# A two-FFN decoder layer with seven-product matrix steps: more of them per chunk, and their closing sums ranked later

## The chip, the cores and the metric

The kernel runs on one core of a Trainium2 chip. The metric is the device time of one execution, in microseconds (us).

## The reference, cut to what matters

One decoder layer over 256 tokens of width 2048, in float32. The two FFNs hold most of the work:

```python
def swiglu(h, w_in, w_out):
    gu = h @ w_in
    gate, up = gu[..., :D_FF], gu[..., D_FF:]
    return (jax.nn.silu(gate) * up) @ w_out

h = h + 0.5 * swiglu(rmsnorm(h, ffn1_norm), ffn1_w_in, ffn1_w_out)
...   # pooling mixer and gated linear attention, h = h + concat(...) @ w_out_mix
h = h + 0.5 * swiglu(rmsnorm(h, ffn2_norm), ffn2_w_in, ffn2_w_out)
return rmsnorm(h, final_norm)
```

D_FF is 5632, so `w_in` is 2048 x 11264 and `w_out` 5632 x 2048.

## The kernel before, in words

**Three matmuls per product.** Every float32 operand is split into a high part (rounded to the matmul's type) and a low part (what is left). A product of two blocks is three matmuls: high x high, low x high and high x low (`three`, line 191, all 128 x 128 by 128 x 512 in the FFNs).

**Steps.** The weights come in loads of 1 MB, each with four blocks of 128 x 512: two blocks of rows by a gate and an up column block (or two column blocks of `w_out`). One load is one step. An ordinary step (S) multiplies the four blocks with the activations of both token halves: eight products, 24 matmuls. A seven-product step (W) is the Winograd form of the same 2 x 2 block product: seven products, 21 matmuls. It pays in vector work. An S step's four blocks go through ScalarE (copy to the high part, line 155) and VectorE (subtract to the low part, line 156). A W step needs seven split blocks (B11, B22, B21 and T1 to T4), and VectorE first forms the T blocks by three subtractions in place (line 179). The sums of activations that a W step multiplies with (`s_f`, `s_z`) are made once per FFN for six of the eight steps.

**Chunks.** `w_in` is worked in 11 chunks of 512 gate and 512 up columns (`first_product`), eight steps each. `KINDS` gives the kinds of the steps by chunk: FFN 1 is named "f", FFN 2 "z". The rows of `CHUNKS` hold for chunks 3 to 10. Between chunks stands a stretch of the second product with `w_out` (`second_product`), as a rule two earlier chunks: four S steps. `GROUPS` sets that alternation.

**PSUM.** A chunk's own sums are two tiles (`ps_fi`, `ps_zi`, one for each token half, in the notation below ps_zi4_0 and ps_zi4_1 for chunk 4). W steps add two more tiles, which collect the products that several outputs share: p16 and p75 in the code, pw_zi4_0 and pw_zi4_1 in names. With them a chunk holds all of PSUM. The second product that follows (`ps_fo`, `ps_zo`) takes the two shared tiles, the first one as its first tile.

**The closing sums.** After the last W step of a chunk `combine` reads the shared tiles: one ScalarE copy (line 297) and four VectorE additions (lines 298 to 301, 128 x 512 each) make `add_fi` or `add_zi`. The copy and the addition of line 298 free the first shared tile. Line 483 then adds the result to the chunk's own sums, lines 490 and 492 gate, line 499 transposes on TensorE, and lines 504 and 505 split the hidden values.

**What sets the order.** The program is written in one stream. A scheduler ranks each instruction by a priority that grows as the code is written, and lays out each engine's order from the ranks and from when it reckons inputs to be ready. At run time each engine takes its instructions in that order; semaphores hold one until its inputs are there. The split blocks lie in rings (22 blocks in all during an FFN), the raw loads in four 1 MB buffers, so ScalarE, VectorE and the loads can run ahead of TensorE only so far.

Of the kernel before, what the change touches and what calls it, by code (L numbers as in the profile page):

```python
# [57 lines left out]


W_PAIRS = (1, 3, 4, 6, 2, 5)  # L60
CHUNKS = ("WWSWWWSS", "WWWWWWSS") * 3 + ("WWSWWWSS",) * 2
KINDS = {
    "f": ("SSSSSSSS", "SSSSSSSS", "WWSWWWSS") + CHUNKS,
    "z": ("SSSSSSSS", "SWSWWWSS", "WWSWWWSS") + CHUNKS,
}
# [10 lines left out]
WIDE = True  # L76
ROW_AT = 7
S_AT = 3
MIX_BLOCKS = 9


@with_exitstack
def layer(ctx: ExitStack, tc: tile.TileContext, io):
# [83 lines left out]
    def s_step(src, parts=1, runs=WIDE):  # L167

        w = load(src, parts=parts).rearrange("p (b c) -> p b c", c=CW)
        b = parts_of(w, SINGLES if parts == 4 else PAIRS if parts == 2 or not WIDE else ALL)  # L170
        return lambda k, n: b[n if k == 0 else 3 - n]

    def w_step(src):

        w = load(src).rearrange("p (b c) -> p b c", c=CW)
        f = dict(zip(("B11", "B22", "B21"), parts_of(w, (slice(0, 1), slice(2, 4)))))

        def less(out, x, y):
            nc.vector.tensor_tensor(out=out, in0=x, in1=y, op=ALU.subtract)  # L179


        less(w[:, 0:2, :], w[:, 1:2, :].broadcast_to([P, 2, CW]), w[:, 0:4:2, :])
        less(w[:, 2, :], w[:, 2, :], w[:, 0, :])
        less(w[:, 3, :], w[:, 3, :], w[:, 2, :])
        f.update(zip(("T1", "T3", "T2", "T4"), parts_of(w, PAIRS)))
        return f

    def three(ps, a, b, start, stop, **kw):

        for i, (x, y) in enumerate(((a[0], b[0]), (a[0], b[1]), (a[1], b[0]))):  # L190
            nc.tensor.matmul(ps, x, y, start=start and i == 0, stop=stop and i == 2, **kw)  # L191

    class Group:
# [66 lines left out]
        def w(self, a, s, b):  # L260

            if self.one is None:
                self.one = [
                    self.psum[self.tags[1]].tile(
                        [P, 2, CW], F32, tag=self.tags[1], name=f"pw_{self.name}_{i}"
                    )
                    for i in range(2)
                ]
                first = True
            else:  # L270
                first = False
            self.left_w -= 1
            last = self.left_w == 0
            p16, p75 = self.one
            for (t, n), x, y in (((0, 0), a(0, 1), b["B21"]), ((0, 1), s["S4"], b["B22"])):
                ps, start, stop = self.target(t, n)
                three(ps, x, y, start, stop)
            three(p16[:, 0, :], a(0, 0), b["B11"], first, last)
            three(p75[:, 1, :], s["S1"], b["T1"], first, last)
            three(p75[:, 0, :], s["S3"], b["T3"], first, last)  # L280
            three(p16[:, 1, :], s["S2"], b["T2"], first, last)
            ps, start, stop = self.target(1, 0)
            three(ps, a(1, 1), b["T4"], start, stop)
            self.n += 1
            if last:
                self.combine()

        def combine(self):

            p16, p75 = self.one  # L290
            self.add = [
                ftmp[0].tile([P, 2, CW], F32, tag=f"add{t}", name=f"add_{self.name}_{t}")
                for t in range(NT)
            ]
            c, d = self.add
            u2 = d[:, 1, :]
            nc.scalar.copy(out=c[:, 0, :], in_=p16[:, 0, :])
            nc.vector.tensor_tensor(out=u2, in0=p16[:, 1, :], in1=c[:, 0, :], op=ALU.add)
            nc.vector.tensor_tensor(out=c[:, 1, :], in0=p75[:, 1, :], in1=u2, op=ALU.add)
            nc.vector.tensor_tensor(out=d[:, 0, :], in0=p75[:, 0, :], in1=u2, op=ALU.add)  # L300
            nc.vector.tensor_tensor(out=d[:, 1, :], in0=p75[:, 1, :], in1=d[:, 0, :], op=ALU.add)
# [133 lines left out]
    def ffn(psum, spool, act, pair, w_in, w_out, row, name, finish, first=None, behind=None):  # L435
# [10 lines left out]
        def a_of(kp):  # L446
            def a(t, k):
                hi, lo = act(2 * kp + k)
                return hi[:, t * P : (t + 1) * P], lo[:, t * P : (t + 1) * P]
            return a  # L450
# [5 lines left out]
        def first_product(c):  # L456
# [4 lines left out]
            for i, kind in enumerate(kinds):  # L461
# [4 lines left out]
                else:  # L466
# [6 lines left out]
                    grp.s(a_of(kp), b)  # L473
                if c == 0 and i >= S_AT:
                    for k in W_PAIRS:
# [207 lines left out]
    mixc = mix_sb.enter_context(tc.tile_pool(name="mixc", bufs=1, reuse_waits="tile"))  # L683
    blk = mix_sb.enter_context(tc.tile_pool(name="blk", bufs=MIX_BLOCKS, reuse_waits="tile"))

# [446 lines left out]
```

## Time and profile before

| | |
|---|---|
| median of 3 runs | 1710.91 us (1709.63 to 1710.96) |
| the profiled execution | 1711.71 us |
| its span, first to last instruction | 1709.9 us |
| TensorE (PE) busy | 1697.0 us, 7732 records |
| weight loads (PEld) busy | 1410.6 us |
| VectorE (DVE) busy | 1375.2 us |
| ScalarE (ACT) busy | 979.7 us |
| GpSimd (POOL) busy | 68.5 us |
| DMA | 365.22 MB, mean 214 GB/s |

Times within the trace count from the start of the span. FFN 1 lies from 0 to about 700 us, the mixer to about 1000 us, FFN 2 from there to the end. [...] In a timeline row stand the start, the duration, the engine, the line, the operation, out<-in, and in brackets the engine's idle time before it with what ended it.

### The profile page before, as it was taken

To read this page: it belongs to the slowest core of one execution; us is meant where nothing else is said; L and a number is where in the kernel's file an instruction comes from. 1 tells how busy PE (TensorE), PEld (TensorE's weight loads), DVE (VectorE), ACT (ScalarE), POOL (GpSimd) and SP (SyncE) were. 2 spreads that over 40 slices of the span, in tenths; PEclk is the share of its full clock that TensorE was granted. 3 is DMA by queue.
4 is the path that set the end of the run, shared out by engine and by line. 5 is a ranking of instruction groups with operands and counts; after the bars stand their busy time and mean duration, and the time that the engine had idled before them with its cause. 6 is when DMAs were issued, how large, how long until landed. Compare 5 with 4: busy or idle time off the path is not lost.

```text
span 1709.9 us, 20097 instructions
## 1 busy us (share of the span) xinstructions
PE 1697.0 (99%) x7732; PEld 1410.6 (82%) x7732; DVE 1375.2 (80%) x1483; ACT 979.7 (57%) x1220; POOL 68.5 (4%) x70
## 2 busy tenths in 40 slices
PE   9999999999999999999999999999999999999997
PEld 7888888888888888888988888888888888888886
DVE  8778899998899986644464677999998988998973
ACT  6655566565566564563454464656556556656542
POOL 0000000000000000000000000000000000000122
PEclk9999999999999999999999999999999999999999
DMA  9845756756756666454564664566667566567671
GB/s 354 335 123 222 265 153 246 271 150 238 252 172 228 239 224 231 171 182 142 191 216 170 213 235 145 190 253 208 210 222 243 176 225 243 182 236 249 200 289 49
DMA packets 60017, 365.22 MB, mean 214 GB/s; under 512 B 6785, under 2 KB 9985, under 8 KB 21266
## 3 DMA queue, kind: packets, MB, share of 16 engines
q1 hardware_dynamic: 51810, 335.61, 53.9%
q0 software_dynamic: 7392, 27.27, 7.5%
q8 instruction: 60, 0.98, 0.2%
q10 hardware_dynamic: 720, 1.07, 0.2%
q14 instruction: 35, 0.29, 0.0%
HBM read 338.75 MB, written 25.17 MB: 213 GB/s over the span
## 4 chain that ended last, share of the span: by engine, by line
PE 99%; issue 0%; ACT 0%; DMA 0%; POOL 0%; DVE 0%; POOLq 0%; ACTq 0%
PE ps_fi L191 19%; PE ps_zi L191 18%; PE ps_fo L191 14%; PE ps_zo L191 14%; PE pw_zi L191 8%; PE pw_fi L191 8%; PE ps_h L191 5%; PE ps_mp L191 3%; PE ps_mv L191 3%; PE ps_mg L191 2%; PE ps_mq L191 1%; PE ps_w_mk L191 1%; PE ps_w_mgr L191 1%; PE ftp L499 1%; PE ztp L499 1%; PE tp_h L428 0%
## 5 line engine op out<-in xcount | busy, mean ns | idle before, releaser
L156 DVE TENSOR_TENSOR ring_lo<-ring_raw,ring_hi 128x1024 fp32r<-128x1024 f32 (+5 forms) x426 | 550.2, 1304 | 213.2 <-ACT ring_hi L155 212.4
L155 ACT CAST ring_hi<-ring_raw 128x1024 fp32r<-128x1024 f32 (+3 forms) x511 | 480.9, 963 | 361.5 <-DMA ring_raw<-in_ffn_w_out 48.1
L179 DVE TENSOR_TENSOR ring_raw<-ring_raw 128x512 f32<-128x512 f32 (+1 forms) x213 | 182.2, 862 | 1.0
L191 PE MATMUL ps_zi<-ring_lo,h_hi 128*128 128x512 f32 x312 | 121.5, 389 | 0.0
L191 PE MATMUL ps_zi<-ring_hi,h_lo 128*128 128x512 f32 x312 | 121.1, 389 | 0.0
L191 PE MATMUL ps_zi<-ring_hi,h_hi 128*128 128x512 f32 x312 | 120.4, 389 | 0.0
L191 PE MATMUL ps_fi<-ring_lo,xT_hi 128*128 128x512 f32 x286 | 112.5, 393 | 0.0
L191 PE MATMUL ps_fi<-ring_hi,xT_lo 128*128 128x512 f32 x286 | 111.4, 392 | 0.0
L191 PE MATMUL ps_fi<-ring_hi,xT_hi 128*128 128x512 f32 x286 | 109.6, 393 | 1.9 <-ACT ring_hi L155 1.9
L191 PE MATMUL ps_fo<-ring_lo,fhi 128*128 128x512 f32 x278 | 109.2, 393 | 0.0
L191 PE MATMUL ps_fo<-ring_hi,flo 128*128 128x512 f32 x278 | 108.5, 392 | 0.0
L191 PE MATMUL ps_fo<-ring_hi,fhi 128*128 128x512 f32 x278 | 107.6, 391 | 0.0
L155 ACT CAST ring_hi<-fring_raw 128x1024 fp32r<-128x1024 f32 (+1 forms) x86 | 79.4, 940 | 46.1 <-DVE fring_raw L179 12.7
L155 ACT CAST zring_hi<-ring_raw 128x1024 fp32r<-128x1024 f32 (+1 forms) x88 | 76.6, 889 | 50.7 <-DVE ring_raw L179 18.3
L155 ACT CAST fring_hi<-ring_raw 128x1024 fp32r<-128x1024 f32 (+1 forms) x84 | 75.8, 927 | 48.9 <-DMA ring_raw<-in_ffn_w_in 10.4
L191 PE MATMUL ps_zo<-ring_hi,zhi 128*128 128x512 f32 x250 | 97.8, 392 | 0.0
L191 PE MATMUL ps_zo<-ring_hi,zlo 128*128 128x512 f32 x250 | 97.6, 391 | 0.0
L191 PE MATMUL ps_zo<-ring_lo,zhi 128*128 128x512 f32 x250 | 97.5, 390 | 0.0
L156 DVE TENSOR_TENSOR ring_lo<-fring_raw,ring_hi 128x1024 fp32r<-128x1024 f32 (+3 forms) x75 | 91.3, 1219 | 6.9 <-ACT ring_hi L155 6.8
L156 DVE TENSOR_TENSOR zring_lo<-ring_raw,zring_hi 128x1024 fp32r<-128x1024 f32 (+3 forms) x77 | 87.5, 1142 | 11.4 <-ACT zring_hi L155 11.4
L156 DVE TENSOR_TENSOR fring_lo<-ring_raw,fring_hi 128x1024 fp32r<-128x1024 f32 (+3 forms) x69 | 86.6, 1265 | 12.2 <-ACT fring_hi L155 12.1
L156 DVE TENSOR_TENSOR ring_lo<-zring_raw,ring_hi 128x1024 fp32r<-128x1024 f32 (+3 forms) x53 | 74.1, 1400 | 6.0 <-ACT ring_hi L155 5.8
(323 smaller groups left out, 3743.2 us busy)
## 6 DMA issues: line engine op xcount, KB each, us to landing
ring_raw<-in_ffn_w_in SPq DMA_DIRECT2D x130, 1024.0 KB, 5.9
ring_raw<-in_ffn_w_out SPq DMA_DIRECT2D x68, 1024.0 KB, 5.1
fring_raw<-in_ffn_w_in SPq DMA_DIRECT2D x22, 1024.0 KB, 7.0
zring_raw<-in_ffn_w_in SPq DMA_DIRECT2D x22, 1024.0 KB, 5.0
ring_raw<-in_w_out_mix SPq DMA_DIRECT2D x16, 1024.0 KB, 4.9
fring_raw<-in_ffn_w_out SPq DMA_DIRECT2D x10, 1024.0 KB, 7.6
zring_raw<-in_ffn_w_out SPq DMA_DIRECT2D x10, 1024.0 KB, 7.4
hd<-half_f POOLq DMA_DIRECT2D x18, 512.0 KB, 8.8
```

Source lines behind the costliest of these rows:

```text
L155: nc.scalar.copy(out=hi[:, j:k, :], in_=src[:, i + j : i + k, :])
L156: nc.vector.tensor_tensor(out=lo, in0=src[:, i : i + n, :], in1=hi.bitcast(F32), op=ALU.subtract)
L179: nc.vector.tensor_tensor(out=out, in0=x, in1=y, op=ALU.subtract)
L191: nc.tensor.matmul(ps, x, y, start=start and i == 0, stop=stop and i == 2, **kw)
L499: nc.tensor.transpose(tp[:, t, k, :], a_t[t][:, k * P : (k + 1) * P], ident)
```

## The change

The last W step's sums are ranked 100 places later, and the kinds of the steps of chunks 3 to 10 become the same for all: six W steps, with an S step between the fifth and the sixth and one at the end. Before, five of those eight chunks had five W steps and three had six. So each FFN has 48 W steps in these chunks where it had 43.

```diff
-CHUNKS = ("WWSWWWSS", "WWWWWWSS") * 3 + ("WWSWWWSS",) * 2
+CHUNKS = ("WWWWWSWS",) * 8
...
+LATER = 100
...
             if last:
+                now = tc.cur_priority
+                tc.cur_priority = now + LATER
                 self.combine()
+                tc.cur_priority = now
```

The lines after the edit stand one line lower from line 79 on, and four lower behind `combine`'s call: line 298 before is line 302 after, 156 is 157, 179 is 180, 191 is 192.

TensorE's order at the end of chunk 4 of FFN 2, before: the last two matmuls into the shared tile pw_zi4_0, the first and last ones of the chunk's own sums that follow, and the first into the second product's tile ps_zo0_2_0, which takes that shared tile's place.

```order
L191 MATMUL pw_zi4_0_8364<-ring_lo_75,s_z2_7003 128x512
L191 MATMUL pw_zi4_0_8364<-ring_hi_74,s_z2_7003 128x512
L191 MATMUL ps_zi4_1_8349<-ring_lo_75,h2_hi2_6276 128x512
L191 MATMUL ps_zi4_1_8349<-ring_hi_74,h2_lo2_6280 128x512
L191 MATMUL ps_zi4_1_8349<-ring_hi_74,h2_hi0_6274 128x512
...
L191 MATMUL ps_zi4_1_8349<-zring_lo_6868,h2_hi3_6277 128x512
L191 MATMUL ps_zi4_1_8349<-zring_hi_6867,h2_lo3_6281 128x512
L191 MATMUL ps_zo0_2_0_8643<-zring_hi_6867,zhi2_7812 128x512
```

The same place after the change.

```order
L192 MATMUL pw_zi4_0_8448<-ring_lo_75,s_z2_7081 128x512
L192 MATMUL pw_zi4_0_8448<-ring_hi_74,s_z2_7081 128x512
L192 MATMUL ps_zi4_1_8435<-ring_lo_75,h2_hi2_6342 128x512
L192 MATMUL ps_zi4_1_8435<-ring_hi_74,h2_lo2_6346 128x512
L192 MATMUL ps_zi4_1_8435<-ring_hi_74,h2_hi3_6343 128x512
...
L192 MATMUL ps_zi4_1_8435<-ring_hi_74,h2_lo3_6347 128x512
L192 MATMUL ps_zo0_2_0_8728<-ring_hi_74,zhi2_7892 128x512
```

Before, 26 matmuls stand between the last one into the shared tile and the first one of the second product; after, 14. Of the 16 chunk ends (chunks 3 to 10 of both FFNs) 15 have 14 after the change, and chunk 3 of FFN 1 has 27; before, the 16 had 26 to 51.

VectorE's order at the same chunk end, before: splits (line 156), then line 298, which frees the shared tile, the other sums, and the addition to the chunk's own first tile (line 483).

```order
L156 TENSOR_TENSOR ring_lo_75<-zring_raw_6866,ring_hi_74 128x1024
L156 TENSOR_TENSOR zring_lo_6868<-zring_raw_6866,zring_hi_6867 128x1024
L156 TENSOR_TENSOR zring_lo_6868<-ring_raw_73,zring_hi_6867 128x2048
L156 TENSOR_TENSOR ring_lo_75<-ring_raw_73,ring_hi_74 128x1024
L156 TENSOR_TENSOR ring_lo_75<-ring_raw_73,ring_hi_74 128x2048
L298 TENSOR_TENSOR add_zi4_1_8555<-pw_zi4_0_8364,add_zi4_0_8554 128x512
L299 TENSOR_TENSOR add_zi4_0_8554<-pw_zi4_1_8365,add_zi4_1_8555 128x512
L300 TENSOR_TENSOR add_zi4_1_8555<-pw_zi4_1_8365,add_zi4_1_8555 128x512
L483 TENSOR_TENSOR ps_zi4_0_8348<-ps_zi4_0_8348,add_zi4_0_8554 128x1024
```

After the change, from the first split whose copy waits for the chunk's last steps.

```order
L157 TENSOR_TENSOR ring_lo_75<-zring_raw_6940,ring_hi_74 128x2048
L157 TENSOR_TENSOR ring_lo_75<-ring_raw_73,ring_hi_74 128x1024 x2
L157 TENSOR_TENSOR zring_lo_6942<-ring_raw_73,zring_hi_6941 128x1024
L157 TENSOR_TENSOR ring_lo_75<-ring_raw_73,ring_hi_74 128x2048
L157 TENSOR_TENSOR ring_lo_75<-zring_raw_6940,ring_hi_74 128x2048
L302 TENSOR_TENSOR add_zi4_1_8669<-pw_zi4_0_8448,add_zi4_0_8668 128x512
L157 TENSOR_TENSOR zring_lo_6942<-ring_raw_73,zring_hi_6941 128x2048
L303 TENSOR_TENSOR add_zi4_0_8668<-pw_zi4_1_8449,add_zi4_1_8669 128x512
L304 TENSOR_TENSOR add_zi4_1_8669<-pw_zi4_1_8449,add_zi4_1_8669 128x512
```

A second 2048-wide split now stands right ahead of the sum that frees the shared tile, and another behind it, ahead of the other sums. In the whole program TensorE has 7643 matmuls where it had 7673, VectorE 82 more two-input instructions and ScalarE 51 more copies; the loads (350 on SP's queue) and GpSimd's transfers (46) are as many as before.

## The prediction

> **What bounds the kernel now.** I read the page first, then the list of who waited for TensorE's inputs, then the windows of single chunk cycles, then the timeline of one chunk end. The page's engine lines and its chain of work:
>
> ```profile
> span 1709.9 us, 20097 instructions
> PE 1697.0 (99%) x7732; PEld 1410.6 (82%) x7732; DVE 1375.2 (80%) x1483; ACT 979.7 (57%) x1220; POOL 68.5 (4%) x70
> ...
> PE 99%; issue 0%; ACT 0%; DMA 0%; POOL 0%; DVE 0%; POOLq 0%; ACTq 0%
> ```
>
> TensorE is the chain. What it waited for in all, from the view of waits for PE alone:
>
> ```profile
> PE ps_fi L191 <- ACT ring_hi L155: 1.9, 1, 1.9
> PE idle L573 <- DVE zeros L570: 1.2, 1, 1.2
> ```
>
> Two waits of 3.1 us together, both in the first microseconds. Between the start and the tail no feeder is ever late, so the time is the number of matmuls times their spacing, and a matmul less is its spacing less, as long as the feeders hold. How near they are stands in the windows. The first five run from one second product's first matmul to the next one's (the second and fourth hold a chunk with six W steps, the others one with five); the last one is nearly all of FFN 2's regular part. Columns: length, then busy time and count for PE, PEld, DVE, ACT, POOL, then the granted clock, the DMA share and GB/s.
>
> ```profile
> 149.61:212.46 62.85, 62.85 (x282) 52.02 (x281) 54.50 (x55) 36.55 (x42) 1.72 (x2) 1.00 0.65 220
> 212.46:274.58 62.12, 62.12 (x279) 51.50 (x278) 59.48 (x63) 39.05 (x44) 1.72 (x2) 1.00 0.64 215
> 274.58:337.42 62.84, 62.84 (x283) 52.02 (x281) 57.65 (x60) 38.79 (x47) 1.72 (x2) 1.00 0.68 228
> 337.42:399.58 62.16, 62.16 (x280) 51.45 (x278) 58.14 (x62) 37.90 (x46) 1.73 (x2) 1.00 0.64 215
> 399.58:462.43 62.85, 62.85 (x283) 52.02 (x282) 55.31 (x53) 36.47 (x41) 1.73 (x2) 1.00 0.65 223
> ...
> 1010.00:1600.00 590.00, 590.00 (x2647) 488.52 (x2646) 536.82 (x570) 352.73 (x420) 16.01 (x17) 1.00 0.62 212
> ```
>
> TensorE is never idle there. VectorE is the next bound: 536.82 of 590.00 us is 91%, and 59.48 of 62.12 (96%) in one cycle with six W steps. ScalarE (60%) and the loads (DMA share 0.62) are far off.
>
> **What the change takes away.** Five S steps become W steps in each FFN, each three matmuls shorter: 2 x 5 x 3 = 30 matmuls, and the order has 7643 for 7673. Their spacing comes from TensorE's timeline at the end of chunk 4 of FFN 2, where 27 steps lie between the first and the last row here:
>
> ```profile
> 1262.83 0.39 PE L191 MATMUL pw_zi<-ring_hi,s_z 128*128 128x512 f32 x1
> 1263.06 0.39 PE L191 MATMUL ps_zi<-ring_lo,h_hi 128*128 128x512 f32 x1
> ...
> 1268.72 0.39 PE L191 MATMUL ps_zi<-zring_hi,h_lo 128*128 128x512 f32 x1
> 1268.95 0.39 PE L191 MATMUL ps_zo<-zring_hi,zhi 128*128 128x512 f32 x1
> ```
>
> 6.12 us / 27 = 0.2267 us each (the 0.39 is the passage of one, overlapped with the next). So 30 x 0.2267 = **6.8 us less**. The cycle windows say the same: 62.84 - 62.16 = 0.68 us for three matmuls. [...]
>
> **What it adds.** The prices of the feeders' work, from the groups with shapes kept apart:
>
> ```profile
> L155 ACT CAST ring_hi<-ring_raw 128x1024 fp32r<-128x1024 f32 x399 | 411.5, 1050 | 296.2 <-DMA ring_raw<-in_ffn_w_out 43.1 <-PE ps_h L191 33.8 <-DVE ring_raw L179 32.6
> L156 DVE TENSOR_TENSOR ring_lo<-ring_raw,ring_hi 128x1024 fp32r<-128x1024 f32 x236 | 286.8, 1221 | 114.0 <-ACT ring_hi L155 113.6
> L156 DVE TENSOR_TENSOR ring_lo<-ring_raw,ring_hi 128x2048 fp32r<-128x2048 f32 x78 | 178.5, 2291 | 68.3 <-ACT ring_hi L155 68.1
> L179 DVE TENSOR_TENSOR ring_raw<-ring_raw 128x512 f32<-128x512 f32 x142 | 96.6, 685 | 0.7
> L179 DVE TENSOR_TENSOR ring_raw<-ring_raw 128x1024 f32<-128x1024 f32 x71 | 86.5, 1218 | 0.3
> L155 ACT CAST ring_hi<-ring_raw 128x512 fp32r<-128x512 f32 x88 | 54.2, 619 | 40.4 <-DMA ring_raw<-in_ffn_w_in 10.2 <-DVE ring_raw L179 5.0 <-DMA ring_raw<-in_ffn_w_out 5.0
> L156 DVE TENSOR_TENSOR ring_lo<-ring_raw,ring_hi 128x512 fp32r<-128x512 f32 x81 | 55.1, 684 | 2.6 <-ACT ring_hi L155 2.5
> ```
>
> VectorE: a W step splits 512 + 3 x 1024 columns (0.68 + 3 x 1.22 = 4.35 us) and subtracts 1024 + 2 x 512 (1.22 + 2 x 0.69 = 2.59 us), 6.94 us in all; an S step is one 2048 split, 2.29 us. Each exchange adds at most 4.65 us of vector work (a little less, since neighbours overlap by 0.1 us). ScalarE: 0.62 + 3 x 1.05 = 3.77 us for 2 x 1.05 = 2.10 us, 1.7 us more. Both are hidden if the cycle holds them. Today's mean cycle is 62.5 us with about 91% x 62.5 = 56.9 us of vector work; from now on each chunk has six W steps where the alternation had five and a half, so 56.9 + 0.5 x 4.65 = 59.2 us in 62.1. That leaves 2.9 us idle, and the window 212.46 to 274.58 already ran without a late input on 62.12 - 59.48 = 2.6 us. ScalarE comes to about 39 us, as it had there. I put the cost of the added work at 0; without that cover it is at most its surplus over the cycle, priced under the rivals. Below nothing it can't be. The loads are as many and as large as before, in SP's order; GpSimd's transfers stay too.
>
> **What it moves.** The sum of line 298 frees the shared PSUM tile for the second product. Today's chunk end with six W steps, on ScalarE and VectorE, same place as above:
>
> ```profile
> 1263.26 0.59 ACT L297 COPY add_zi<-pw_zi 128x512 f32<-128x512 f32 x1 [4.11 <-PE pw_zi L191]
> ```
>
> ```profile
> 1259.18 2.29 DVE L156 TENSOR_TENSOR ring_lo<-ring_raw,ring_hi 128x2048 fp32r<-128x2048 f32 x1 [1.12 <-ACT ring_hi L155]
> 1263.88 0.69 DVE L298 TENSOR_TENSOR add_zi<-pw_zi,add_zi 128x512 f32<-128x512 f32 x1 [2.41 <-ACT add_zi L297]
> 1264.61 0.69 DVE L299 TENSOR_TENSOR add_zi<-pw_zi,add_zi 128x512 f32<-128x512 f32 x1
> ```
>
> From the last matmul into the tile (1262.83) to the end of line 298 (1264.57) it is 1.74 us, and TensorE needs the tile 6.12 us after that matmul: 4.4 us to spare. VectorE stood still for 2.41 us in front of line 298, with the later splits behind it. After the change TensorE needs the tile 15 spacings after that matmul, 3.40 us, so 1.66 us are to spare if VectorE is free. Is it? In FFN 2's new order six splits stand ahead of the sum: 2048, 1024, 1024, 1024, 2048, 2048, that is 3 x 2.29 + 3 x 1.22 = 10.5 us, or 10.0 with their overlaps. The copy for the first waits, by the semaphores, for a product 51 places ahead of the last one into the tile, 11.56 us earlier. That copy takes 0.43 us to start (1263.26 - 1262.83) and 1.05, so the splits can run from 1.5 us on, with some 0.9 us of waiting for copies between them, and end 12.4 us after that product. The sum's own copy ends at 11.56 + 0.43 + 0.59 = 12.6. So the sum runs from 12.6 to 13.3, and TensorE needs the tile at 66 x 0.2267 = 15.0: **1.6 us to spare**. FFN 1's order is tighter. Six splits (1024, 1536, 512, 2048, 512, 1536) run back to back from 2.5 us after the product that lets their copies begin (0.43 and two copies of 1.05); with a 1536 at (1.22 + 2.29) / 2 = 1.75 us they are 1.22 + 2 x 1.75 + 2 x 0.68 + 2.29 = 8.4 us, 7.9 with overlaps. The sum ends at 2.5 + 7.9 + 0.7 = 11.1 and TensorE needs the tile 53 places behind that product, at 12.0: **0.9 us to spare**, and there VectorE, not the copy, comes last. The other sums (lines 299 to 301) and the 2048 split ahead of them have at least 57 spacings, 12.9 us. Line 483's addition, the gating and the transposes keep 37 or more matmuls (8.4 us) between them and the next user of their tiles. I take the cost of the move at 0.
>
> Sum: 1711.71 - 6.8 = 1704.9 us for the profiled execution, which lay 0.8 us above the median of the runs. For the median 1710.91 - 6.8 = **1704.1 us**. A change of 0.2%, 3.4 us, is about what a measurement of this kernel can tell from none.
>
> **The rivals.**
>
> *VectorE's queue becomes the bound at the chunk ends, and the kernel is slower.* TensorE's cover at a chunk end shrinks from 6.1 to 11.8 us (27 to 52 spacings) to 3.4 us, while the vector work ahead of the releasing sum grows. If VectorE reaches FFN 1's last six splits later than the copies allow, TensorE stands still for what exceeds 0.9 us. [...] In cycles: today's VectorE is idle for 62.5 - 56.9 = 5.6 us of each, waiting for copies and sums. If 3.5 us of that can't be used, the cycle is 59.2 + 3.5 = 62.7 us, 0.2 over today's, and if all can't, 64.8. Over 16 cycles that is 3 us to 37 us slower than before, 1714 to 1748. It decides from 62.5 - 59.2 = 3.3 us of idle that stays. Against it: the window with 2.6 us idle, and that the new S step between the fifth and the sixth W step lets VectorE catch up 24 x 0.2267 - 2.29 = 3.2 us. For it: that window is one cycle between two lighter ones. 0.13.
>
> *The gain is eaten.* The same mechanism, smaller: late by 0.2 to 0.45 us at each of 16 chunk ends, 3.4 to 6.8 us back, 1707.5 to 1710.9. A load that lands late would act in the same way. 0.15.
>
> *Part of it is eaten*: 1 to 3.4 us over all chunk ends, 1705 to 1707.5. 0.12.
>
> That the change doesn't shorten the program is excluded by the count of matmuls.
>
> **How the numbers follow.** The forecast, no stall or under 1 us in all, has 0.60. The low end is the lowest run less the gain, 1709.63 - 6.8 = 1702.8, since idle time at the start and in the tail isn't touched. The high end takes in the partly eaten gain and most of the eaten one, 1709.5. Faster by over 0.2%: 0.60 + 0.12 = 0.72; within 0.2%: 0.15; slower: 0.13.
>
> **What would show it.** Right: about 6.8 us less PE busy time; still no PE wait of note in the regular part; cycles of 62.1 us everywhere; DVE busy 59 to 60 us in each; 1.6 us between line 302's end and the second product's first matmul in FFN 2, 0.9 in FFN 1. Wrong: PE idle before `ps_fo` or `ps_zo` released by line 302 (the first rival, at its place), or before `ps_fi` and `ps_zi` released by line 157 (VectorE late inside the chunk, so that the mean cycle has been misjudged), or a DVE share that doesn't rise.

## The result, and the profile after

The changed kernel takes 1722.63 us (median of 6 runs, 1721.71 to 1733.23) beside 1710.27 us of the kernel before in the same session (6 runs, 1709.19 to 1711.88): the ratio is 1.0082, with a 95% interval of 1.0058 to 1.0107. It is **slower by 0.8%**, where 0.4% faster was forecast. The profiled execution took 1722.41 us, of which the span is 1720.6, 10.7 us longer than before.

The page's engine lines and its chain of work, after the change:

```profile
span 1720.6 us, 20112 instructions
PE 1691.7 (98%) x7702; PEld 1403.9 (82%) x7702; DVE 1413.7 (82%) x1565; ACT 997.9 (58%) x1271; POOL 64.7 (4%) x70
...
PE 78%; DMA 8%; DVE 8%; issue 3%; ACT 2%; SPq 0%; POOL 0%; ACTq 0%; POOLq 0%; DVEq 0%
```

Before, the chain was TensorE for 99%. Now 22% of it is something else: transfers, VectorE, ScalarE and short times of issue. What TensorE waited for, from the view of waits for PE:

```profile
PE ps_fo L192 <- DVE add_fi L302: 11.4, 6, 3.4
PE ps_zo L192 <- DVE add_zi L302: 3.1, 2, 1.6
PE ps_fi L192 <- ACT ring_hi L156: 1.8, 1, 1.8
PE ps_fi L192 <- DVE ring_lo L157: 1.6, 3, 0.7
```

Eight waits at chunk ends, 14.5 us, all for the sum that frees the shared PSUM tile, and most of them in FFN 1. The windows from the second product's first matmul behind chunk 2 to the one behind chunk 10, FFN 1 and then FFN 2, before:

```profile
149.61:650.22 500.61, 500.61 (x2241) 414.58 (x2239) 454.15 (x459) 300.99 (x351) 15.29 (x18) 1.00 0.65 222
1143.96:1644.56 500.60, 500.60 (x2241) 414.48 (x2239) 458.44 (x460) 300.99 (x351) 24.78 (x20) 1.00 0.66 224
```

And after:

```profile
149.24:660.66 511.42, 500.04 (x2225) 412.41 (x2224) 471.57 (x494) 309.41 (x376) 15.28 (x18) 1.00 0.65 216
1154.57:1655.11 500.54, 497.44 (x2226) 411.73 (x2224) 472.81 (x488) 308.97 (x360) 19.33 (x20) 1.00 0.67 222
```

FFN 1 lost 10.8 us and FFN 2 gained 0.1. Fifteen matmuls less are 3.4 us in each, so FFN 1 gave back 14.2 us and FFN 2 3.3. VectorE's work grew alike in both, to 472 us in eight cycles, 59 us in each, as forecast. Two cycles of the changed kernel, the fifth of those eight in FFN 1 and the fifth in FFN 2:

```profile
400.96:466.78 65.82, 62.42 (x278) 51.43 (x278) 59.34 (x63) 39.48 (x49) 1.72 (x2) 1.00 0.65 217
1405.02:1467.11 62.09, 62.09 (x279) 51.51 (x278) 59.23 (x62) 38.70 (x45) 1.72 (x2) 1.00 0.66 217
```

The same vector work (59.34 and 59.23 us) takes 65.82 us in one and fits into 62.09 in the other. So VectorE's amount of work is not what separates them. What stands ahead of the stall at 466.78 us shows in the chain of waits (start, duration, what), read from the window 440 to 467:

```profile
443.33 1.15 DVE ring_lo L157
...
444.50 7.03 DMA ring_raw<-in_ffn_w_in
...
452.51 1.05 ACT ring_hi L156
...
453.58 2.30 DVE ring_lo L157
...
455.90 6.33 DMA ring_raw<-in_ffn_w_out
...
462.78 1.57 ACT ring_hi L156 x2
...
466.05 0.69 DVE add_fi L302
...
466.78 0.79 PE ps_fo L192
```

This is a loop. VectorE's last read of one raw buffer ends at 444.48, the next load into that buffer is issued at 444.50 and lands 7.03 us later, ScalarE copies it, VectorE splits it until 455.88, the load after that, again into the same buffer, is issued at 455.90, and so on. The releasing sum stands behind splits that wait for such loads, and TensorE waits for the sum. ScalarE's waits for loads in this stretch (window 211 to 660 us):

```profile
ACT ring_hi L156 <- DVE ring_raw L180: 40.0, 21, 3.7
ACT ring_hi L156 <- DMA ring_raw<-in_ffn_w_in: 32.3, 12, 5.0
ACT fring_hi L156 <- DMA ring_raw<-in_ffn_w_out: 22.1, 13, 3.9
ACT fring_hi L156 <- DMA fring_raw<-in_ffn_w_in: 18.8, 6, 3.9
```

The three rows of loads make 73 us in some seven cycles, and with two small groups it is 79. The landing of a load there (smallest, median, largest; line 136, the same window):

```profile
DMA to landing us min/median/max: 4.8/7.0/10.4
```

In FFN 2's regular part the median is 5.4. Worked out from the issues, the landings and VectorE's counts of FFN 1's 78 regular loads (215 to 650 us): a buffer is taken again 0.03 us after it is free, and stays taken 21.1 us, 6.6 for the landing and 14.5 until VectorE's last read. Twelve loads a cycle over four buffers make 3 x 21.13 = 63.4 us, about the mean of FFN 1's cycles (511.42 / 8 = 63.9). That the two are alike is arithmetic and no evidence. When every buffer is taken again as soon as it is free, four buffers are each held for a third of the cycle, whichever of the two sets the other. The kernel before issues its loads 0.03 us after a buffer is free as well (212 to 650 us), and there the same sum gives 4 x 62.58 / 12 = 20.9 us, with a TensorE that never waits. Which of the two sets the other is for the experiments to say.

### The profile page after: what moved, and what is told of

Read it like the earlier page. It is cut to its first block, busy times and chain, and to the rows that moved or that the text cites. A ratio compares the mean times of both kernels' runs of the same rounds, so it can differ in the third digit from the quotient of the medians.

```text
span 1720.6 us, 20112 instructions
## 1 busy us (share of the span) xinstructions
PE 1691.7 (98%) x7702; PEld 1403.9 (82%) x7702; DVE 1413.7 (82%) x1565; ACT 997.9 (58%) x1271; POOL 64.7 (4%) x70
## 4 chain that ended last, share of the span: by engine, by line
PE 78%; DMA 8%; DVE 8%; issue 3%; ACT 2%; SPq 0%; POOL 0%; ACTq 0%; POOLq 0%; DVEq 0%
PE ps_zi L192 14%; PE ps_zo L192 12%; PE ps_fo L192 11%; PE ps_fi L192 10%; PE pw_zi L192 8%; PE ps_h L192 5%; PE pw_fi L192 4%; DVE ring_lo L157 4%; DMA ring_raw<-in_ffn_w_in 3%; PE ps_mp L192 3%; PE ps_mv L192 3%; DMA ring_raw<-in_ffn_w_out 2%; DMA fring_raw<-in_ffn_w_in 2%; ACT ring_hi L156 2%; PE ps_mg L192 2%
## 5 line engine op out<-in xcount | busy, mean ns | idle before, releaser
L157 DVE TENSOR_TENSOR ring_lo<-ring_raw,ring_hi 128x1024 fp32r<-128x1024 f32 (+6 forms) x487 | 580.3, 1204 | 198.0 <-ACT ring_hi L156 197.3
L180 DVE TENSOR_TENSOR ring_raw<-ring_raw 128x512 f32<-128x512 f32 (+1 forms) x267 | 228.0, 860 | 0.5
L157 DVE TENSOR_TENSOR zring_lo<-ring_raw,zring_hi 128x512 fp32r<-128x512 f32 (+3 forms) x93 | 111.4, 1200 | 14.3 <-ACT zring_hi L156 14.3
L157 DVE TENSOR_TENSOR ring_lo<-zring_raw,ring_hi 128x1024 fp32r<-128x1024 f32 (+2 forms) x65 | 94.1, 1447 | 15.3 <-ACT ring_hi L156 15.1
L192 PE MATMUL ps_fo<-ring_hi,fhi 128*128 128x512 f32 x240 | 94.7, 400 | 11.4 <-DVE add_fi L302 11.4
L156 ACT CAST ring_hi<-zring_raw 128x1024 fp32r<-128x1024 f32 (+1 forms) x85 | 82.9, 989 | 35.1 <-DMA zring_raw<-in_ffn_w_out 11.7
L192 PE MATMUL pw_zi<-ring_hi,s_z 128*128 128x512 f32 x294 | 103.0, 389 | 0.0
L192 PE MATMUL pw_fi<-ring_hi,s_f 128*128 128x512 f32 x274 | 95.9, 389 | 0.0
L192 PE MATMUL ps_zi<-ring_hi,h_lo 128*128 128x512 f32 x232 | 90.5, 390 | 0.0
L192 PE MATMUL ps_zi<-ring_lo,h_hi 128*128 128x512 f32 x232 | 90.3, 389 | 0.0
L192 PE MATMUL ps_zi<-ring_hi,h_hi 128*128 128x512 f32 x232 | 89.3, 390 | 0.0
```

What stands on the lines that cost most here:

```text
L156: nc.scalar.copy(out=hi[:, j:k, :], in_=src[:, i + j : i + k, :])
L157: nc.vector.tensor_tensor(out=lo, in0=src[:, i : i + n, :], in1=hi.bitcast(F32), op=ALU.subtract)
```

## The experiments

Three theories stood at the start. A: six seven-product steps in every chunk leave VectorE too little room in FFN 1, where loads land late. B: the later rank puts the releasing sum behind too much. C: the place of the last ordinary steps cuts TensorE's cover to 15 spacings. D and E came after the first four runs, R and S after the next three.

**E1, the step kinds without the later rank.**

```diff
-CHUNKS = ("WWSWWWSS", "WWWWWWSS") * 3 + ("WWSWWWSS",) * 2
+CHUNKS = ("WWWWWSWS",) * 8
```

> The new step kinds with the sums at their old rank; TensorE's order and its cover of 15 spacings are those of the changed kernel, only VectorE's and ScalarE's orders differ. Theory A (too little room: with six seven-product steps in every chunk VectorE is busy 59.3 of 62.1 us, and in FFN 1, where a load lands 7 to 9 us after its issue, that is not enough): still slower than before, 1717 to 1726 us, with 10 us or more of TensorE waiting for the sum in FFN 1. Theory B (the later rank is the cause: the releasing sum stands behind a 2048-wide split): the loss goes, 1703 to 1706 us. Theory C (the place of the last ordinary steps cuts TensorE's cover to 15 spacings, and the wait appears there): as A, 1717 to 1726 us; this run does not tell A from C.

Measured: 1721.6 us against 1710.8 before, ratio 1.0068 (1.0054 to 1.0083), as slow as the whole change. TensorE waits 8.6 us for the sum in FFN 1 (theory A had 10 or more) and 4.8 in FFN 2. The loss is there without the later rank, so B falls. FFN 2 is not free of it: its eight cycles take 503.89 us here, 6.7 over the 497.2 that 15 matmuls less would leave, all of it in the first two and the last one.

**E2, the later rank without the step kinds.** The old `CHUNKS`, and `combine` ranked 100 later as in the change.

> The old step kinds with the sums ranked 100 places later; TensorE's cover stays 27 to 52 spacings. A and C: no change from before, 1709 to 1712 us. B: slower than before, by up to the 16 us of waits that the changed kernel shows if the rank alone made them, 1715 to 1726 us.

Measured: 1709.3 us, ratio 0.9994 (0.9986 to 1.0003). No change. The rank costs nothing under the old kinds, and E1 next to the whole change shows that it saves nothing under the new ones.

**E3, six seven-product steps and then both ordinary ones.**

```diff
+CHUNKS = ("WWWWWWSS",) * 8
```

> Six seven-product steps in each of the eight chunks and both ordinary steps at the end, sums at their old rank; as many matmuls as the changed kernel (7643), but TensorE's cover between the last matmul into the shared tile and the second product is 27 to 39 spacings instead of 15. Theory A (amount of vector work): as slow as the changed kernel in FFN 1, 1715 to 1724 us. Theory C (cover): the forecast's 6.8 us come out, 1703 to 1706 us. Theory B says the same as C here, since the rank is the old one.

Measured: 1716.22 us, ratio 1.0033 (1.002 to 1.0046). Half of E1's loss (10.8 us, here 5.4) goes with the longer cover and half stays, so neither A nor C holds alone. Where TensorE waits has changed too:

```profile
PE ps_fo L191 <- DVE ring_lo L156: 3.4, 2, 1.7
PE ps_zo L191 <- DVE ring_lo L156: 2.2, 4, 0.9
...
PE ps_fo L191 <- DVE add_fi L301: 1.2, 3, 0.7
```

It waits for late splits of the second product, not for the sum of line 298. FFN 1's cycles are 62.17, 62.16, 66.26, 62.14, 62.16, 66.29, 62.14 and 62.19 us. The two long ones start at the two chunk ends whose cover is 28 spacings; the other six start at ends with 39 or 45. It looks as if the feeders fell behind and the longer covers took it up, but whether lateness piles up over several chunks or the order at these two ends makes it was not separated.

**E4, the whole change in FFN 2 alone.** `OLD` holds the rows of `CHUNKS` from before.

```diff
-    "f": ("SSSSSSSS", "SSSSSSSS", "WWSWWWSS") + CHUNKS,
+    "f": ("SSSSSSSS", "SSSSSSSS", "WWSWWWSS") + OLD,
...
-                tc.cur_priority = now + LATER
+                later = self.name[0] == "z"
+                if later:
+                    tc.cur_priority = now + LATER
                 self.combine()
```

> The change in FFN 2 alone; FFN 1 keeps the old kinds and ranks. In the changed kernel FFN 2's cycles were 62.1 us but for two, and nearly all of the loss lay in FFN 1. If what costs is FFN 1's own state (late loads, theory A), this one has 15 matmuls less and about 2 us of waits: 1707 to 1709.5 us, faster than both kernels. If the loss comes with the step order or rank as such (B, C), FFN 2 would show waits of several us: 1711 to 1716 us.

Measured: 1707.31 us, ratio 0.9982 (0.9973 to 0.999). Faster than both kernels, and below the one before by the 15 matmuls' 3.4 us (3.5 measured). FFN 2's eight cycles:

```profile
1141.18:1638.25 497.07, 497.07 (x2225) 411.90 (x2224) 472.28 (x488) 305.17 (x365) 19.55 (x20) 1.00 0.66 222
```

No wait at all, with 472.28 us of vector work and covers of 16 to 28 spacings. So a cycle of 62.1 us does hold 59 us of vector work and a short cover, and four raw buffers can feed it: its eight cycles are 62.1 to 62.2 us. It is not quite the changed kernel's FFN 2, whose cover was 15 and whose first and last cycles stalled. From here on the question is what is different in FFN 1, where nearly all of the loss lies.

**E5, FFN 1 entering the ring of split blocks one block later.** Here I took the place in the ring as the difference (theory D): FFN 1's chunks start at block 3, FFN 2's at block 4.

```diff
+SKIP = {"f": 1, "z": 21}
...
         more_ring(spool, MORE_RAW, MORE_RING, f"{name}ring")
+        for _ in range(SKIP[name]):
+            blocks.take(1)
```

> The changed kernel with FFN 1 entering the ring of split blocks one block further on, so that each of its regular chunks starts at block 4 of the ring (0 to 21) as in FFN 2, not at block 3; FFN 2 stays at 4. Same matmuls (7643), same step kinds, same rank of the sums, TensorE's cover 15 spacings as in the changed kernel. Theory D (the place in the ring decides: at an odd place the wrap at blocks 16 and 22 cuts pairs into single blocks and an ordinary step into 1536 + 512 columns, so FFN 1's vector and scalar orders run late at the chunk end; the work is the same 59.3 us in both FFNs): FFN 1's stalls go, its cycles become 62.1 us as in FFN 2, 1704 to 1708 us. Theory E (FFN 1's loads land later, 6.8 to 7.2 us against 5.3 to 5.6 in FFN 2, for a reason of their own, and the sums follow them): FFN 1's stalls stay, 1717 to 1724 us.

Measured: 1733.38 us, ratio 1.014 (1.012 to 1.0159). FFN 1 became worse, not better: 17.0 us of waits for the sum. The time lies outside what either theory gave.

**E6 and E7, FFN 2 at FFN 1's place, and both at the best place.** The same edit with 0 and 21, and with 13 and 21.

> The changed kernel with FFN 2 shifted to block 3 of the ring, where FFN 1 is; FFN 1 untouched. Theory D: FFN 2 now stalls before ps_zo at its chunk ends as FFN 1 does, another 8 to 14 us: 1727 to 1737 us. Theory E: FFN 2 keeps its cycles of 62.1 us, 1719 to 1724 us.

> Both FFNs shifted so that their chunks start at block 16, where the wrap cuts the fewest splits (31 pieces a cycle instead of 33 at block 4 and 34 at block 3, so about 0.2 to 0.3 us less vector work). Theory D: no stall in the regular part of either FFN, the forecast's 6.8 us come out, 1702.5 to 1706 us. Theory E: FFN 1's stalls stay, 1715 to 1724 us.

Measured: 1723.77 us, ratio 1.0078 (1.0059 to 1.0098), and 1722.28 us, ratio 1.0069 (1.0055 to 1.0083). FFN 2 ran most of its regular cycles in 62.1 us at blocks 3, 4 and 16; FFN 1 stalled at all three. Theory D falls. What E said of these two runs came out, and it leaves open why the loads are late. The place in the ring changes the orders and with them how much FFN 1 loses, but not that it loses.

**E8, a fifth raw buffer.** Now the loop seen in the chain (theory R). The space comes from two split blocks.

```diff
-MORE_RAW = 1
-MORE_RING = 6
+MORE_RAW = 2
+MORE_RING = 4
```

> The changed kernel with five raw 1 MB buffers instead of four; the space comes from the ring of split blocks, 20 instead of 22. Theory R (the raw buffers are the loop: in the changed kernel's FFN 1 each of them is taken again 0.03 us after it is freed and stays taken 21.1 us, 6.6 for the landing and 14.5 until VectorE's last read, and 12 loads a cycle over four buffers make 3 x 21.1 = 63.3 us where TensorE needs 62.1): with five buffers the loop allows 12 x 21.1 / 5 = 50.7 us, FFN 1's stalls go, 1704 to 1709 us. Theory S (the orders of ScalarE and VectorE themselves, or VectorE's 59.3 us, are too long whatever the buffers): FFN 1's cycles stay above 63 us, 1717 us or more, as in the control with 20 blocks and four raw buffers.

Measured: 1710.53 us, ratio 1.0004 (0.9996 to 1.0013). The total is a little above what R expected, but FFN 1 did as R said. The windows of both FFNs:

```profile
148.70:647.00 498.30, 497.64 (x2225) 411.68 (x2224) 472.67 (x493) 307.64 (x374) 15.32 (x18) 1.00 0.66 222
1139.16:1642.03 502.87, 499.99 (x2225) 412.56 (x2224) 473.80 (x492) 307.65 (x361) 18.87 (x20) 1.00 0.65 218
```

FFN 1: 498.30 us where the change had 511.42, with as much vector work (472.67) and the cover still 15 spacings at six of its eight chunk ends. ScalarE's waits for loads in FFN 1 (window 211 to 660) went from 79 us to 10:

```profile
ACT ring_hi L156 <- DMA ring_raw<-in_ffn_w_out: 6.5, 4, 3.7
ACT ring_hi L156 <- DVE ring_raw L180: 5.3, 4, 1.7
ACT ring_hi L156 <- DMA fring_raw<-in_ffn_w_out: 3.6, 3, 1.7
```

FFN 2 stands 5.8 us above E4's instead, with one wait of 2.6 us in the middle of a chunk for a split (line 157). It had been free of waits with four buffers and 22 blocks, and now has two blocks less. E9's FFN 2, also with 20 blocks, stands at 503.08 us.

The expectation's 50.7 us was never a length of this loop. With five buffers a load is still issued 0.03 us after a buffer is free, so that each is held 5 x 62.29 / 12 = 26.0 us. What is gone is the copies' waiting for loads.

**E9, the control: 20 split blocks, four raw buffers.** `MORE_RING = 4` alone.

> The control for the fifth raw buffer: the changed kernel with 20 split blocks instead of 22 and the four raw buffers as they are. Two blocks less let the splits run less far ahead; the chunk starts wander through the ring and TensorE's cover is 26 to 28 spacings at about half the chunk ends. R and S: not faster than the changed kernel by more than the longer covers give, 1714 to 1730 us, with stalls in FFN 1.

Measured: 1716.14 us, ratio 1.0035 (1.0021 to 1.0049), FFN 1's window 505.25 us, with ScalarE waiting 76 us for loads there. The covers are longer in this order (26 to 28 spacings at five of the eight chunk ends), which may be why less is lost; the waits for loads stay. Of two kernels with 20 blocks, the one with the fifth buffer is rid of them, though its covers are shorter.

**E10, the change with five raw buffers in FFN 1 only.** FFN 2 keeps four buffers and 22 blocks and enters the ring where E4's FFN 2 did.

```diff
+MORE_RAW = {"f": 2, "z": 1}
+MORE_RING = {"f": 4, "z": 6}
+SKIP = {"f": 0, "z": 11}
```

> The whole change (new kinds and later sums in both FFNs, 7643 matmuls), with five raw buffers and 20 split blocks in FFN 1 only; FFN 2 keeps four and 22, and enters the ring where the run with the change in FFN 2 alone entered it, so that its orders from chunk 4 on are that run's. Theory R (FFN 1's raw buffers were the loop): FFN 1 as with five buffers (cycles of 62.1 to 62.2 us, under 1 us of stalls), FFN 2 without a stall as in that run, so all 30 matmuls come out: 1702.5 to 1705 us, faster than both kernels. Theory S (the orders or VectorE's share are too long for FFN 1 and five buffers only happened to suit): stalls come back, 1708 us or more.

Measured: **1704.54 us** (6 runs, 1703.65 to 1705.8), ratio 0.997 (0.9959 to 0.9981). Faster than both kernels. The page's engine lines, and what TensorE waits for in FFN 1 (window 20 to 660):

```profile
span 1704.0 us, 20131 instructions
PE 1689.9 (99%) x7702; PEld 1404.2 (82%) x7702; DVE 1412.8 (83%) x1563; ACT 996.8 (58%) x1279; POOL 62.1 (4%) x70
```

```profile
PE ps_fo L193 <- DVE add_fi L303: 0.7, 1, 0.7
PE ps_fi L193 <- DVE ring_lo L158: 0.6, 1, 0.6
```

VectorE's busy time, 1412.8 us, is the changed kernel's 1413.7. The second row lies ahead of the regular part, and FFN 2 has no wait. The waits are gone, the work is not.

**E11, five raw buffers in FFN 1 under the old kinds.**

> The old kinds and the old rank of the sums, with five raw buffers and 20 split blocks in FFN 1: what the buffer does without the change. Theory R: the old kernel never waited for a load, so a fifth buffer has nothing to give, 1708.5 to 1712 us. If it gave 2 us or more here, the fifth buffer would be a gain of its own and not the release of what the change ran into.

Measured: 1709.69 us, ratio 0.9998 (0.9989 to 1.0007). The fifth buffer is no gain of its own. It releases what the change ran into. Over all runs with the new kinds in FFN 1, the seven with four buffers lost 8 to 25 us there against 497.2, in several different orders, and the two with five, which share one order, lost 1.1 and 1.2.

## Why the prediction was wrong

**The gain was right.** 30 matmuls at 0.2267 us, 6.8 us. With the loop released (E10) the kernel comes to 1704.54 us where 1704.1 was forecast, and 5.8 us below the 1710.38 us of its session; the 1.0 us that lacks is near the 0.7 us that FFN 1 still waits at one chunk end.

**The vector work was right in size**: 59.2 us a cycle forecast, 59 us a cycle measured in both FFNs. In FFN 2 the cycle was 62.1 to 62.3 us in six of eight chunks; the first and the last took 63.9 and 63.8.

**The step that failed** is the one that put the cost of the added work at 0 because "both are hidden if the cycle holds them", together with "the loads are as many and as large as before, in SP's order", and the DMA share of 0.62 as "far off". Each engine's work was held against the cycle by itself. Nothing was asked about the loop that joins them: buffer free, load, landing, copy, splits, buffer free. Its length is a time, not a busy share. A seven-product step holds its buffer until the last split of its T blocks. In the changed kernel's FFN 1, around the stall at 466.78, its loads issued at 419.36 and 436.19 kept their buffers 29.9 and 20.9 us (until the next load into the same buffer was issued), those of the ordinary steps, issued at 427.57 and 444.50, 15.2 and 11.4. The change has one more such step in five of eight chunks, and in FFN 1 four buffers then no longer kept up with TensorE's 62.1 us (E8 to E11). The kinds alone don't do it, since E4's FFN 2 ran them through four buffers without a wait. FFN 1 gave back 14.2 us for a term that had been put at 0. Before, ScalarE waited for loads too, 51 us in the window 212 to 650:

```profile
ACT ring_hi L155 <- DMA ring_raw<-in_ffn_w_out: 21.4, 11, 4.6
ACT ring_hi L155 <- DMA fring_raw<-in_ffn_w_in: 9.7, 3, 4.3
ACT fring_hi L155 <- DMA ring_raw<-in_ffn_w_in: 9.5, 5, 3.2
ACT ring_hi L155 <- DMA ring_raw<-in_ffn_w_in: 5.6, 3, 2.9
```

TensorE did not feel these waits (busy for all 500.61 us of its FFN 1 window); that the longer cover and the lighter chunks in between hid them is likely, but no run shows it alone. The rows were in the trace, and I took ScalarE's 60% as slack. SP's order was not the old one either: in the new order a load of `w_out` stands ahead of the chunk's last load of `w_in`. That is not the cause: E4's FFN 2 has this order and no wait, and E3 keeps the old one and still lost 8.3 us in FFN 1.

**The margins.** FFN 1's 0.9 us at the chunk end were worked out from when the copies may begin by TensorE's progress, with the loads in place. Where they were not, as at 462.25 (a copy that had waited 3.85 us for a load), the sum ended 3.4 us after TensorE had come to need it. FFN 2's 1.6 us were 1.1 to 1.3 at five of its chunk ends, 0.5 at one, and it came too late at the two others, by 1.6 and 1.5 us. In E10, where the copies hardly wait for loads, FFN 1's six ends with a cover of 15 spacings had 0.07 to 1.66 us to spare, so 0.9 was a fair size for the case without late loads.

**The rivals.** The first one named the place (line 302 ahead of `ps_fo`), the sign and the range (1714 to 1748) and had 0.13. Its cause, idle time of VectorE that can't be used, is the right half: VectorE stood waiting for copies that waited for loads, which it left out. The second rival carried the other half in a sentence, "a load that lands late would act in the same way", and gave it no price.

**The cost of the move** was put at 0. For the rank of the sums E2 and E1 agree. The shorter cover cost nothing once the loop was released: FFN 1's one wait in E10's regular part, 0.7 us, stands at a chunk end with a cover of 27. With late loads it was the place where TensorE stood.

**What stays open**: why FFN 1 and not FFN 2. Both have the same kinds, buffers and sizes; TensorE's, ScalarE's and VectorE's orders differ between them in the second half of a cycle, and the median load lands in 7.0 against 5.4 us. A slow landing alone is not it: in E10's FFN 2 the median is 6.3 us, with four buffers and no wait of TensorE. Whether the order makes the loads collide or the collisions only go with it wasn't separated. Nor is FFN 2 safe, as its 6.7 us in E1 show. That in FFN 1 five buffers and 20 blocks are enough while four and 20 aren't is shown, though with orders that differ somewhat.

## What to carry to other kernels

A prefetch loop (buffer free, load, landing, copy, last read) can be the bound while no engine's busy share shows it. In the changed kernel's FFN 1 VectorE was busy for 471.57 of 511.42 us and ScalarE for 309.41, at a DMA share of 0.65, and the seven-product steps looked at kept their buffers 29.9 and 20.9 us where the ordinary ones kept them 15.2 and 11.4. The time that a buffer is held does not tell: where each load is issued as soon as its buffer is free, it is buffers times cycle over loads by arithmetic, 20.9 us before the change and 26.0 in E8's FFN 1, though TensorE hardly waited in either. Look at what the copies wait for, and then try one buffer more: the waits for loads went from 79 us to 10, and TensorE's with them. Such waits alone prove nothing either, since the kernel before had 51 us of them and lost no time. Look at how cycle times run over several chunks, not at one: the changed FFN 1 began with two cycles of 62.17 us, as forecast, and its sixth took 66.16. And a kernel in which two halves do the same work at different speeds is the best place to look, since whatever they share can't be the whole cause.

## What was not expected of the hardware

**A stall cost more than its length.** After the wait that ends at 466.78 us TensorE's matmuls start 0.427 us apart, not 0.227. Its timeline in the changed kernel, with the first matmul as it ends the wait:

```profile
466.78 0.79 PE L192 MATMUL ps_fo<-ring_hi,fhi 128*128 128x512 f32 x1 [3.40 <-DVE add_fi L302]
467.37 0.63 PE L192 MATMUL ps_fo<-ring_lo,fhi 128*128 128x512 f32 x1
467.80 0.63 PE L192 MATMUL ps_fo<-ring_hi,flo 128*128 128x512 f32 x1
468.23 0.63 PE L192 MATMUL ps_fo<-ring_hi,fhi 128*128 128x512 f32 x1
```

The granted clock in the windows behind it:

```profile
466.70:468.00 1.30, 1.22 (x3) 1.03 (x4) 1.26 (x4) 0.03 (x1) 0.00 (x0) 0.50 0.96 378
468.00:470.00 2.00, 2.00 (x7) 1.57 (x6) 2.00 (x2) 0.17 (x1) 0.00 (x0) 0.57 0.98 332
470.00:472.00 2.00, 2.00 (x11) 1.62 (x10) 2.00 (x4) 1.98 (x3) 0.00 (x0) 1.00 0.80 234
```

The trace's clock record has 0.50 from 466.32 to 469.74 us, 3.41 us, and 1.00 before and behind it. From 466.78 on that is 2.96 us at half the rate, so some 1.5 us are lost on top of the wait, an estimate from these numbers.

The length of a wait alone does not tell whether this comes with it. Of the changed kernel's eight waits for the sum two came with such a stretch: that of 3.40 us and that of 1.83 us, which ends at 660.66 (0.50 from 660.88 to 664.30 us). That of 2.40 us, which ends at 532.94, did not, nor did the five of 1.04 to 1.64 us. In E3 a wait of 1.70 us that ends at 277.30 did, with 0.50 in the window 277.90 to 279.00. In E8 one of 2.59 us did not: behind 1512.66 its matmuls start 0.23 to 0.24 us apart. The kernel before has one such stretch too, from 753.21 to 756.62 us in the mixer, with TensorE busy for all of the 3.42 us ahead of it. What makes the clock fall is not shown by these runs.

**Landing times.** Loads of the same 1 MB took 4.8 to 10.4 us to land in the changed kernel's FFN 1 (211 to 660 us). The mean DMA share of FFN 1's window (149.24 to 660.66 us) was 0.65, which did not tell how long a single load took.
